# Three pairs of accumulator banks in turn, instead of two, in the feed-forwards of 512 tokens

## The chip, the cores and the metric

The kernel runs on one core of one Trainium2 chip. The metric is device microseconds of one execution of the whole program, taken as the median of several runs. Engines are named as in the profile: PE (TensorE matmuls), PEld (its weight loads), DVE (VectorE), ACT (ScalarE), POOL (GpSimd), SP (SyncE, which issues DMAs).

## The reference, cut to what matters

The reference is a four-layer network over 512 tokens of width 1024 in float32: a gated delta-rule layer, a dilated attention layer, and two layers of a second block that mixes neighbourhood attention, spatial gating and grouped attention, the first of them over 512 tokens and 256 context tokens. Every layer ends in a feed-forward with 2816 hidden columns. Cut down, the feed-forward is:

```
a, b = h @ w_in[:, :2816], h @ w_in[:, 2816:]     # "g" and "u" halves
x = x + (silu(a) * b) @ w_out                     # block 2 adds gains and norms
```

The second block also needs a modulation: for each of its two layers, `silu(c) @ w_mod[l] + b_mod[l]`, a vector times a 1024 x 6144 matrix, which depends on nothing but the inputs.

## The kernel before

Matrices are float32, and every operand is split into a high and a low part, so that a product is three matmuls (high by high, high by low, low by high). A matmul covers 128 rows, 128 contracted and up to 512 columns. Weights stream in slabs: SP loads one into `wraw`, ACT casts it to `whi`, POOL subtracts to make `wlo`. There are four `whi`/`wlo` pairs (names ending a and b), and a slab's pair is free for the next cast once PE has used it.

There are four feed-forwards, all in `ffn_core`. Three have 512 tokens (`nb` is 4): `ffn(0)`, `ffn(1)` and the one in `layer2(1)`. The one in `layer2(0)` has 768 tokens (`nb` is 6). In this text they are the first, second, fourth and third. The 22 hidden tiles of 128 columns are worked in three groups of 8, 8 and 6 (`FFN_GROUPS`). A group first computes its hidden tiles: a tile is 48 matmuls of 512 columns, 24 for `g` and 24 for `u`, into one pair of banks. Then `post` runs for the tile: ACT takes a tanh of `g` into `th`, DVE does a scalar_tensor_tensor and a tensor_tensor (both out `th`, in `th` and the banks) and so frees the pair, ACT casts to `hh` and POOL subtracts to `hl`. After the tiles comes the group's output: two halves of 512 columns, each with four accumulators (one for each block of 128 tokens), over n/2 weight slabs `c`. One slab for one block is six matmuls. An accumulator is added to `x` by `evac`, which is DVE work, and is free then. In the last group the second half goes through `tail`, block by block, with 18 matmuls each.

PSUM has eight banks: a ring of two for `psM`, two for `psS`, and two tiles of two banks for `psB`. In the feed-forwards of 512 tokens the hidden tiles take `psB` tiles in turn, each output half takes both `psB` tiles (`accs`: blocks 0 and 1 in one, 2 and 3 in the other), and the tail takes the two `psM` banks in turn. A `psB` tile comes free when all that was read from it has been read.

While the first two feed-forwards run, `modulation` computes the modulation on DVE, as a stream of lower priority: a 128 x 1024 piece of `w_mod` arrives in `mw` (a ring of three, issued from ACT's queue) and DVE multiplies and adds it into `macc`, 48 pieces in all, each for two vectors in the first feed-forward and for one or two in the second. After each eight pieces DVE transposes and reduces `macc` to `mpart`, PE does a small matmul of `mpart` into a `psS` bank, and DVE reads that into `modc`.

The order of the instructions on each engine is set when the program is built. `Weave` keeps an estimated clock for each engine, with costs of its own (`cost`), and steps a stream when the estimate says that its input is there; `Ring.get` advances the streams until a bank has been released in that order. A scheduler behind it places the instructions of each engine by a timeline of its own. Every engine then runs its queue in that order.

In the profile every instruction stands under line L138, the helper that records operations, so the rows are told apart by tile names: `b` is a `psB` tile, `m` a `psM` bank, `s` a `psS` bank.

Of the kernel before, what the change touches and what calls it, by code (L numbers as in the profile page):

```python
# [274 lines left out]
class Ring:  # L275
# [18 lines left out]
    def get(self):  # L294
        if self.held >= self.n:
            self.w.until(self.has)
            self.w.t["PE"] = max(self.w.t["PE"], self.time)
        return self._tile()
# [84 lines left out]
class Build:  # L383
# [108 lines left out]
            mm(ps, xh(k0 + k), lo[:, k], start=False, stop=last and k == nk - 1)  # L492
        self.w.tick()

    def gemm_b(self, arr, plan, keys, blocks, post, prio=0, base=0):

        P = PLANS[plan][0]
        n = P[keys[0]][4]
        held = [None] * len(keys)
        out = []  # L500
        for i, (b, rows, xh, xl, pre) in enumerate(blocks):
            if pre is not None:
                self.w.join(pre)
            ps = self.psM.get()[:rows, :n]
            for c, key in enumerate(keys):
                if held[c] is None:
                    held[c] = self.slabs.get(arr, key)
                self.mm_b(ps, xh, xl, held[c], P[key][1] - base, c == 0, c == len(keys) - 1)
                if i == len(blocks) - 1:
                    self.slabs.done(held[c])  # L510
            out.append(self.w.spawn(post(b, ps), prio))
        return out
# [591 lines left out]
    def accs(self, n, kinds="bbmm"):  # L1104
# [15 lines left out]
                out += [(t[:, :512], rel), (t[:, 512:], rel)]  # L1120
        return out

    def next_norm(self, side, row):

        es = ExitStack()
        self.n_act = getattr(self, "n_act", 0) + 1
        pool = self.open(es, f"act{self.n_act}", 1, side)
        xh = pool.tile([128, 8, 512], F32R, name="xh")
        xl = pool.tile([128, 8, 512], F32R, name="xl")
        gain = pool.tile([128, 1024], F32, name="row")  # L1130
        self.nc.sync.dma_start(gain, row.partition_broadcast(128))
        spare = FixedRing(self.w, [self.cx[:, 0], self.cx[:, 1]])
        return {"es": es, "xh": xh, "xl": xl, "st": [None] * 4, "gain": gain,
                "gen": lambda b: self.norm_rms(b, gain, xh, xl, self.nat, spare if b > 1 else None)}

    def tail(self, arr, plan, keys, blocks, evac, before, nxt, base=0):

        def post(b, ps):
            yield from evac(b, ps)
            if before:  # L1140
                yield before[b]
            nxt["st"][b] = self.w.spawn(nxt["gen"](b), 1)

        self.gemm_b(arr, plan, keys, blocks, post, 0, base)
        self.w.until(lambda: all(s is not None for s in nxt["st"]))


# [1 line left out]
    def ffn_core(self, wi, wo, segs, pre, setup, evac, nxt, grid=None):  # L1149

        nc, w, v = self.nc, self.w, self.nc.vector
        nb = sum(n for _, _, n in segs) // 128
        posts, mem = {}, {}

        def hidden(gi):
            if "one" not in mem:
                mem["one"] = setup()
                mem["th"] = Ring(w, mem["one"], "th", [128, nb * 128], 2)  # L1160
            if gi not in mem:
                mem[gi] = [(mem["one"].tile([128, 8, t], F32R, name=f"hh{i}", tag=f"hh{i}"),
                            mem["one"].tile([128, 8, t], F32R, name=f"hl{i}", tag=f"hl{i}"))
                           for i, (_, _, t) in enumerate(segs)]
            return mem[gi]

        def post(j, kk, pb, px, hs):
            rth = mem["th"]
            th = yield from rth.take()
            ps = [(pb[:, :512], pb[:, 512:], slice(0, 512))]  # L1170
            if px is not None:
                ps.append((px[:, :256], px[:, 256:], slice(512, 768)))
            for pg, _, t in ps:
                nc.scalar.activation(th[:, t], pg, AF.Tanh, scale=0.5)
            yield
            for pg, _, t in ps:
                v.scalar_tensor_tensor(th[:, t], th[:, t], 1.0, pg, ALU.add, ALU.mult)
            for _, pu, t in ps:
                v.tensor_mul(th[:, t], th[:, t], pu)
            self.psB.rel()  # L1180
            if px is not None:
                self.psM.rel()
            yield
            for (hh, hl), (_, _, t) in zip(hs, ps):
                oh, ol, s = hh[:, kk], hl[:, kk], th[:, t]
                if grid is not None:
                    g = "p (c s n) -> p n s c", "p (n s c) -> p n s c"
                    g = g if grid == "to" else g[::-1]
                    oh, ol = (x.rearrange(g[0], s=2, n=4) for x in (oh, ol))
                    s = s.rearrange(g[1], s=2, n=4)  # L1190
                nc.scalar.copy(oh, s)
                self.sub(ol, s, oh.bitcast(F32), "pool")
            rth.rel()

        def outs(half, pb, px, c0, c1):

            o = []
            if c0 < 512:
                xh, xl, _ = segs[0]
                c = slice(c0, min(c1, 512))  # L1200
                o.append((pb[:, 512 * half + c.start:512 * half + c.stop], lambda k: xh[:, k, c],
                          lambda k: xl[:, k, c]))
            if c1 > 512:
                yh, yl, n = segs[1]
                o.append((px[:, n * half:n * half + n], lambda k: yh[:, k], lambda k: yl[:, k]))
            return o

        def units(js, gi, k0, cuts):
            pbs = [(self.psB.get(), self.psM.get() if len(segs) > 1 else None) for _ in js]
            sl = {}  # L1210
            end = cuts[-1][1]
            for c0, c1, need in cuts:
                w.join(*need)
                for j, (pb, px) in zip(js, pbs):
                    for half, m in enumerate("gu"):
                        if (m, j) not in sl:
                            sl[m, j] = self.slabs.get(wi, (m, j))
                        self.mm_a(sl[m, j], outs(half, pb, px, c0, c1))
                        if c1 == end:
                            self.slabs.done(sl[m, j])  # L1220
                    if c1 == end:
                        posts[j] = w.spawn(post(j, j - k0, pb, px, hidden(gi)), 0)

        first = [(0, 256, pre[:2]), (256, 512, pre[2:4])]
        if nb > 4:
            first.insert(0, (512, 768, pre[4:]))
        for gi, (k0, n) in enumerate(FFN_GROUPS):
            js = list(range(k0, k0 + n))
            if not gi:
                units(js[:2], gi, k0, first)  # L1230
                js = js[2:]
            for j in js:
                units([j], gi, k0, [(0, 128 * nb, [])])

            def blk(b, hs=mem[gi]):
                (hh, hl), t = (hs[0], b * 128) if b < 4 else (hs[1], b * 128 - 512)
                return (lambda k: hh[:, k, t:t + 128]), (lambda k: hl[:, k, t:t + 128])

            ev = {}
            last = gi == len(FFN_GROUPS) - 1  # L1240
            for h in range(1 if last else 2):
                acc = self.accs(nb)
                order = list(range(nb))
                for c in range(n // 2):
                    w.join(*(posts.pop(j, None) for j in (k0 + 2 * c, k0 + 2 * c + 1)))
                    slab = self.slabs.get(wo, (gi, h, c))
                    for b in order:
                        self.mm_b(acc[b][0], *blk(b), slab, 2 * c, c == 0, c == n // 2 - 1)
                        if c == n // 2 - 1:
                            def ev0(gi=gi, b=b, h=h, acc=acc):  # L1250
                                yield from evac(gi, h, b, acc[b][0])
                                acc[b][1]()
                            ev[b] = w.spawn(ev0(), 0)
                    self.slabs.done(slab)
            if last:
                nxt = nxt()

                def ev1(b, ps):
                    yield from evac(gi, 1, b, ps)
                    self.psM.rel()  # L1260

                order = ([4, 5] if nb > 4 else []) + [0, 1, 2, 3]
                blocks = [(b, 128, *blk(b), None) for b in order]
                self.tail(wo, "ffn_out", [(gi, 1, c) for c in range(n // 2)], blocks, ev1, ev, nxt, k0)
        return nxt

    def ffn(self, i, after):
# [1308 lines left out]
```

## Time and profile before

| what | value |
|---|---|
| median of 3 runs | 3430.48 us (3426.53 to 3433.2) |
| profiled execution, its time | 3435.41 us |
| profiled execution, its span | 3433.6 us |
| PE busy | 3123.7 us, 91% of the span |
| DVE busy | 1735.3 us, 51% |
| ACT busy | 1257.0 us, 37% |
| POOL busy | 1440.1 us, 42% |
| mean granted TensorE clock | 0.947 of full speed |

The profiled execution's time is 4.93 us above the median and 1.81 us above its span. The first feed-forward runs from about 440 to 835 us of the span, the second from about 1205 to 1605 us, the third from about 2100 to 2630 us, the fourth from about 3050 to 3417 us.

### The profile page before, as it was taken

What the parts mean: (1) busy time and instruction counts of PE and PEld (TensorE: products, weight loads), DVE (VectorE), ACT (ScalarE), POOL (GpSimd) and SP (SyncE); (2) the same over time, 40 slices, a digit from 0 to 9 for tenths busy, and PEclk for the clock granted to TensorE, in tenths of its full rate; (3) what the DMA queues carried; (4) which work ended last, traced back from release to release, by engine and by line L of the source; (5) the groups of instructions that cost most, each with busy time, mean ns of one, the idle gap of its engine ahead of it and who ended that gap; (6) DMA issues with size and microseconds to landing.
All of it is one profiled execution on the core that took longest, in us unless ns stands there. A gap on an engine that the chain in (4) does not pass through costs nothing.

```text
span 3433.6 us, 44377 instructions
## 1 busy us (share of the span) xinstructions
PE 3123.7 (91%) x16596; PEld 2696.9 (79%) x16596; DVE 1735.3 (51%) x4221; ACT 1257.0 (37%) x2542; POOL 1440.1 (42%) x987
## 2 busy tenths in 40 slices
PE   7889888999999979999899897999998799869998
PEld 5678767777998767788788777888886789758886
DVE  6975598543464697213644755121015855751113
ACT  4443322222454422333455635212122555543322
POOL 2313344554323245555523325434445534355555
PEclk9989989999999989999999899999999899889999
DMA  3111255432222267323101212111111111242221
GB/s 106 63 33 62 87 178 172 158 122 95 68 63 68 74 210 244 124 94 118 51 24 44 74 41 80 62 65 65 62 67 53 52 39 54 66 122 94 98 98 68
DMA packets 99449, 301.82 MB, mean 88 GB/s; under 512 B 18673, under 2 KB 26017, under 8 KB 99233
## 3 DMA queue, kind: packets, MB, share of 16 engines
q1 hardware_dynamic: 74000, 236.36, 20.3%
q10 hardware_dynamic: 25232, 62.62, 5.7%
q8 instruction: 131, 2.15, 0.3%
q14 instruction: 86, 0.70, 0.1%
HBM read 290.98 MB, written 7.95 MB: 87 GB/s over the span
## 4 chain that ended last, share of the span: by engine, by line
PE 67%; DVE 23%; issue 4%; ACT 3%; DMA 2%; POOL 1%; ACTq 0%; SPq 0%; DVEq 0%; POOLq 0%
PE b L138 37%; PE m L138 24%; PE s L138 6%; DVE macc L138 5%; DVE rs_t L138 4%; DVE x L138 2%; DVE four L138 1%; ACT xn L138 1%; DMA mw<-w_mod 1%; DVE w2k L138 1%; DVE qrs L138 1%; DVE cx L138 1%; DVE tmp L138 1%; DVE T L138 1%; DVE th L138 1%
## 5 line engine op out<-in xcount | busy, mean ns | idle before, releaser
L138 POOL TENSOR_TENSOR wloa<-wrawa,whia 128x1024 fp32r<-128x1024 f32 (+2 forms) x164 | 391.9, 2391 | 617.8 <-ACT whia L138 375.3
L138 DVE SCALAR_TENSOR_TENSOR th<-th,b 128x512 f32<-128x512 f32 x88 | 60.3, 685 | 720.3 <-ACT th L138 720.3
L138 POOL TENSOR_TENSOR wlob<-wrawa,whib 128x1024 fp32r<-128x1024 f32 (+1 forms) x123 | 297.7, 2423 | 301.2 <-ACT whib L138 191.2
L138 ACT CAST whia<-wrawa 128x1024 fp32r<-128x1024 f32 (+2 forms) x164 | 168.3, 1027 | 401.8 <-PE b L138 162.0
L138 PE MATMUL b<-xh,whib 128*128 128x512 f32 (+1 forms) x768 | 288.6, 381 | 24.2 <-DVE th L138 16.8
L138 PE MATMUL b<-xh,whia 128*128 128x512 f32 (+1 forms) x768 | 286.7, 379 | 14.1 <-DVE th L138 12.1
L138 PE MATMUL b<-xl,whia 128*128 128x512 f32 (+1 forms) x768 | 285.2, 377 | 2.0 <-POOL xl L138 2.0
L138 PE MATMUL b<-xl,whib 128*128 128x512 f32 (+1 forms) x768 | 286.7, 379 | 0.0
L138 DVE SCALAR_TENSOR_TENSOR macc<-mw,cv,macc 128x1024 f32<-128x1024 f32 x140 | 247.9, 1812 | 16.1 <-DMA mw<-w_mod 15.6
L138 ACT CAST whib<-wrawa 128x1024 fp32r<-128x1024 f32 (+1 forms) x123 | 125.7, 1022 | 327.8 <-PE b L138 164.5
L138 POOL TENSOR_TENSOR wloa<-wrawb,whia 128x1024 fp32r<-128x1024 f32 (+2 forms) x61 | 141.6, 2321 | 189.5 <-ACT whia L138 120.2
L138 PE MATMUL m<-xh,whia 128*128 128x512 f32 (+2 forms) x520 | 188.3, 367 | 23.6 <-DVE T L138 10.1
L138 POOL TENSOR_TENSOR wlob<-wrawb,whib 128x1024 fp32r<-128x1024 f32 (+1 forms) x61 | 149.8, 2456 | 131.3 <-ACT whib L138 85.4
L138 POOL TENSOR_TENSOR hl<-th,hh 128x512 fp32r<-128x512 f32 (+1 forms) x110 | 151.8, 1389 | 101.4 <-ACT hh L138 97.0
L138 PE MATMUL b<-xh,wlob 128*128 128x512 f32 (+1 forms) x768 | 194.0, 373 | 0.0
L138 PE MATMUL b<-xh,wloa 128*128 128x512 f32 (+1 forms) x768 | 192.2, 372 | 0.0
L138 PE MATMUL m<-xl,whia 128*128 128x512 f32 (+2 forms) x520 | 184.9, 360 | 3.0 <-POOL xl L138 2.9
L138 PEld LDWEIGHTS b<-xh,whib 128*128 128x128 f32 x768 | 148.0, 193 | 47.3 <-issue 11.9
L138 PEld LDWEIGHTS b<-xh,whia 128*128 128x128 f32 x768 | 147.1, 191 | 36.4 <-issue 13.6
L138 PE MATMUL m<-whib,xh 128*128 128x512 f32 (+3 forms) x432 | 162.6, 379 | 13.8 <-ACT xh L138 12.8
L138 PE MATMUL m<-whia,xh 128*128 128x512 f32 (+3 forms) x440 | 170.8, 392 | 4.6 <-ACT xh L138 2.8
L138 PE MATMUL m<-whia,xl 128*128 128x512 f32 (+3 forms) x440 | 167.3, 383 | 0.4 <-DVE xl L138 0.3
(459 smaller groups left out, 8025.7 us busy)
## 6 DMA issues: line engine op xcount, KB each, us to landing
mw<-w_mod ACTq DMA_DIRECT2D x96, 512.0 KB, 4.3
wrawa<-ffn_w_in SPq DMA_DIRECT2D x60, 512.0 KB, 3.3
wrawa<-w_ffn_in SPq DMA_DIRECT2D x56, 512.0 KB, 3.3
wrawa<-gdn_w_in SPq DMA_DIRECT2D x32, 512.0 KB, 3.3
wrawb<-w_ffn_in SPq DMA_DIRECT2D x32, 512.0 KB, 3.3
wrawa<-w_ffn_out SPq DMA_DIRECT2D x32, 512.0 KB, 3.3
wrawb<-ffn_w_in SPq DMA_DIRECT2D x28, 512.0 KB, 3.3
wrawa<-ffn_w_out SPq DMA_DIRECT2D x28, 512.0 KB, 3.3
```

What stands on the lines that cost most here:

```text
L138: r = f(*a, **k)
```

## The change

Where `nb` is 4, the two `psM` banks become a third pair that takes turns with the two `psB` tiles. `pair()` hands out the pairs in a fixed rotation that runs on from one feed-forward to the next. Hidden tiles, both output halves and the tail all draw from it. A pair drawn for two accumulators is released when both have been added to `x`; in the tail, too, blocks 0 and 1 share a pair and so do blocks 2 and 3. The feed-forward of 768 tokens keeps its banks.

```diff
-    def gemm_b(self, arr, plan, keys, blocks, post, prio=0, base=0):
+    def gemm_b(self, arr, plan, keys, blocks, post, prio=0, base=0, get=None):
...
-            ps = self.psM.get()[:rows, :n]
+            ps = (get(b) if get else self.psM.get())[:rows, :n]
...
+    def pair(self):
+
+        i = self.turn = (getattr(self, "turn", -1) + 1) % 3
+        if i < 2:
+            t = self.psB.get()
+            return (t[:, :512], t[:, 512:]), self.psB.rel
+
+        def rel():
+            self.psM.rel()
+            self.psM.rel()
+
+        return (self.psM.get(), self.psM.get()), rel
+
+    def banks(self):
+
+        while True:
+            ps, rel = self.pair()
+            left = [2]
+
+            def half(left=left, rel=rel):
+                left[0] -= 1
+                if not left[0]:
+                    rel()
+
+            for p in ps:
+                yield p, half
...
-    def tail(self, arr, plan, keys, blocks, evac, before, nxt, base=0):
+    def tail(self, arr, plan, keys, blocks, evac, before, nxt, base=0, get=None):
...
-        self.gemm_b(arr, plan, keys, blocks, post, 0, base)
+        self.gemm_b(arr, plan, keys, blocks, post, 0, base, get)
...
-            ps = [(pb[:, :512], pb[:, 512:], slice(0, 512))]
+            (pg, pu), rel = pb
+            ps = [(pg, pu, slice(0, 512))]
...
-            self.psB.rel()
+            rel()
...
+        def wide():
+
+            if len(segs) == 1:
+                return self.pair(), None
+            t = self.psB.get()
+            return ((t[:, :512], t[:, 512:]), self.psB.rel), self.psM.get()
+
...
-                o.append((pb[:, 512 * half + c.start:512 * half + c.stop], lambda k: xh[:, k, c],
+                o.append((pb[0][half][:, c], lambda k: xh[:, k, c],
...
-            pbs = [(self.psB.get(), self.psM.get() if len(segs) > 1 else None) for _ in js]
+            pbs = [wide() for _ in js]
...
-                acc = self.accs(nb)
+                if nb > 4:
+                    acc = self.accs(nb)
+                else:
+                    bank = self.banks()
+                    acc = [next(bank) for _ in range(nb)]
...
+                bank, rels = self.banks(), {}
+
+                def get(b):
+                    if nb > 4:
+                        rels[b] = self.psM.rel
+                        return self.psM.get()
+                    ps, rels[b] = next(bank)
+                    return ps
+
                 def ev1(b, ps):
                     yield from evac(gi, 1, b, ps)
-                    self.psM.rel()
+                    rels[b]()
...
-                self.tail(wo, "ffn_out", [(gi, 1, c) for c in range(n // 2)], blocks, ev1, ev, nxt, k0)
+                self.tail(wo, "ffn_out", [(gi, 1, c) for c in range(n // 2)], blocks, ev1, ev, nxt, k0, get)
```

## Rows read from the trace of the kernel before

**Rows 1.** The page: busy time of each engine.

```profile
PE 3123.7 (91%) x16596; PEld 2696.9 (79%) x16596; DVE 1735.3 (51%) x4221; ACT 1257.0 (37%) x2542; POOL 1440.1 (42%) x987
```

**Rows 2.** Waits of PE, 430 to 860 us, then 1190 to 1640 us.

```profile
PE b L138 <- DVE th L138: 23.4, 8, 5.7
...
PE b L138 <- DVE x L138: 2.2, 2, 1.3
...
PE b L138 <- DVE th L138: 19.3, 4, 7.2
...
PE b L138 <- DVE x L138: 5.8, 1, 5.8
```

**Rows 3.** Windows: length, then PE, PEld, DVE, ACT, POOL busy, granted clock, DMA.

```profile
455.00:557.00 102.00, 84.67 (x391) 69.59 (x390) 100.59 (x69) 25.42 (x32) 52.23 (x23) 0.92 0.58 191
...
3064.00:3409.00 345.00, 345.00 (x1581) 288.43 (x1581) 60.15 (x88) 106.91 (x113) 200.85 (x97) 1.00 0.27 92
```

**Rows 4.** Timeline of PE, first feed-forward: start, us, instruction, idle before and releaser.

```profile
470.77 0.76 PE L138 MATMUL b<-xh,whib 128*128 128x512 f32 x1 [5.67 <-DVE th L138]
...
474.30 0.40 PE L138 MATMUL b<-xh,whib 128*128 128x512 f32 x1
...
509.90 0.76 PE L138 MATMUL b<-xh,whia 128*128 128x512 f32 x1 [3.71 <-DVE th L138]
...
553.38 0.77 PE L138 MATMUL b<-whib,hh 128*128 128x512 f32 x1 [4.88 <-DVE th L138]
...
578.61 0.47 PE L138 MATMUL b<-whib,hh 128*128 128x512 f32 x1 [1.27 <-DVE x L138]
...
626.00 0.47 PE L138 MATMUL b<-xh,whib 128*128 128x512 f32 x1 [3.22 <-DVE th L138]
...
637.62 0.47 PE L138 MATMUL b<-xh,whia 128*128 128x512 f32 x1 [0.46 <-DVE th L138]
...
703.90 0.50 PE L138 MATMUL b<-whib,hh 128*128 128x512 f32 x1 [2.40 <-DVE th L138]
...
720.25 0.31 PE L138 MATMUL s<-mpart,quart 128*32 128x16 f32 x8 [2.87 <-DVE mpart L138]
...
721.45 0.76 PE L138 MATMUL b<-whib,hh 128*128 128x512 f32 x1 [0.89 <-DVE x L138]
```

**Rows 5.** The chain that ended last: an undisturbed stretch of hidden tiles.

```profile
746.10 71.22 PE b L138 x314
```

**Rows 6.** Timeline of DVE, first feed-forward: posts of tiles 5, 6 and 7.

```profile
536.52 0.68 DVE L138 TENSOR_TENSOR th<-th,b 128x512 f32<-128x512 f32 x1
...
552.55 0.68 DVE L138 TENSOR_TENSOR th<-th,b 128x512 f32<-128x512 f32 x1
...
556.08 0.69 DVE L138 TENSOR_TENSOR th<-th,b 128x512 f32<-128x512 f32 x1
569.28 0.24 DVE L138 SCALAR_TENSOR_TENSOR modc<-s,bm 128x8 f32<-128x8 f32 x2 [12.51 <-PE s L138]
```

**Rows 7.** Timeline of PE, second feed-forward.

```profile
1249.27 0.77 PE L138 MATMUL b<-xh,whib 128*128 128x512 f32 x1 [7.25 <-DVE th L138]
...
1289.42 0.77 PE L138 MATMUL b<-xh,whia 128*128 128x512 f32 x1 [5.24 <-DVE th L138]
...
1338.34 0.80 PE L138 MATMUL b<-whib,hh 128*128 128x512 f32 x1 [6.59 <-DVE th L138]
...
1383.28 0.77 PE L138 MATMUL b<-xh,whib 128*128 128x512 f32 x1 [5.79 <-DVE x L138]
```

**Rows 8.** Timeline of DVE, second feed-forward: posts of tiles 6 and 7.

```profile
1323.23 0.68 DVE L138 TENSOR_TENSOR th<-th,b 128x512 f32<-128x512 f32 x1
...
1337.60 0.69 DVE L138 TENSOR_TENSOR th<-th,b 128x512 f32<-128x512 f32 x1
```

**Rows 9.** The costliest groups, then the timeline of ACT.

```profile
L138 DVE SCALAR_TENSOR_TENSOR macc<-mw,cv,macc 128x1024 f32<-128x1024 f32 x140 | 247.9, 1812 | 16.1 <-DMA mw<-w_mod 15.6
...
525.06 1.05 ACT L138 CAST whia<-wrawa 128x1024 fp32r<-128x1024 f32 x1 [4.47 <-DVE macc L138]
```

## The prediction, made before the change was built

> **What bounds the kernel now.** I read the page first. PE is busy for 91% of the span and no other engine for more than 51% [rows 1], so a gain has to come out of PE's idle time or its clock. Then I asked for PE's waits in the stretches of the feed-forwards, since the change touches nothing else. "PE b <- DVE th" is PE standing before a `psB` bank that a tile's post on DVE has not yet freed, and "PE b <- DVE x" is the same before an `evac`. In the first feed-forward they are 23.4 + 2.2 = 25.6 us, in the second 19.3 + 5.8 = 25.1 us [rows 2], 50.7 us in all. The fourth has none: PE is busy 345.00 of 345.00 us there [rows 3]. So only the first two can gain, and these are the two in which the modulation runs on DVE.
>
> The timeline of PE shows where the waits stand and that a long one costs more than itself. After 5.67 us of waiting at 470.77, eight matmuls take 474.30 - 470.77 = 3.53 us [rows 4], and in an undisturbed stretch eight take 8 x 71.22/314 = 1.81 us [rows 5]. So the clock is at its lower level for a moment and 1.7 us more is lost. The first matmul after a wait shows it by its own length: 0.76 to 0.80 us at the lower level, 0.47 to 0.50 otherwise [rows 4, 7]. Eight of these waits end in a matmul of the long kind [rows 4, 7], so the clock costs 8 x 1.7 = 13.6 us. The most that the change could give back is 50.7 + 13.6 = 64 us.
>
> Last I looked at what the late engine does meanwhile. From 455 to 557 us DVE is busy 100.59 of 102.00 us [rows 3]. The waits are thus not a hiccup that a deeper queue swallows: for these 100 us DVE, with the modulation in its queue, is the slower engine. One multiply-add into `macc` takes 1.81 us on average [rows 9], where the planner counts on 120 + 1.04 x 1024 = 1185 ns. The posts stand in DVE's queue behind them.
>
> **The change part by part.** It adds no arithmetic, no copy and no DMA. A third pair lets PE begin a tile when the post three tiles back is done instead of two, so it may lead DVE by one tile more. An undisturbed tile is 48 x 71.22/314 = 10.9 us [rows 5]. I assume that DVE keeps its order and, where it is full, its times.
>
> *First feed-forward, first group.* The rotation gives the group's eight tiles pairs 0,1,2,0,1,2,0,1, its first half pairs 2 and 0, its second half 1 and 2. PE is through tiles 0 and 1 at 470.77 - 5.67 = 465.1 [rows 4]. Tiles 2 to 5 then need 4 x 10.9 us, to 508.7. Tile 6 needs post 3, which released tile 5 at 509.9 [rows 4], 1 us later, and with tile 7 and 0.5 us for modulation matmuls the tiles end near 532. Blocks 0 and 1 of the first half wait for post 5 instead of 6: 537.2 instead of 553.23 [rows 6]. Blocks 2 and 3 wait for post 6 instead of 7: 553.23 instead of 556.77. So the waits saved inside the tiles come back in front of blocks 2 and 3, because DVE gets to post 6 no earlier. What remains is the work left at 553.3. Before, the half ended at 578.61 - 1.27 = 577.3 [rows 4]. After, if PE's order goes slab by slab, 12 of 96 matmuls are done and 84 follow at 0.227 us, plus 1.7 us for the clock: 553.3 + 19.1 + 1.7 = 574.1, a gain of 3.2. If blocks 0 and 1 run ahead by some 30 matmuls, as they do now, 66 remain: 553.3 + 15.0 + 1.7 = 570.0, a gain of 7.3. I take 5.
>
> *Its second half and second group.* The second half draws tile 7's pair, free since post 7, so the 1.27 us before it go. Tiles 10 and 11 waited 3.22 and 0.46 us for posts 8 and 9 [rows 4]. They now need posts 7 and 8 or an accumulator pair long empty, so these go as well: 5 + 1.27 + 3.22 + 0.46 = 10. DVE drains in between, so nothing returns here. In the group's output the 2.40 us at 703.90 go, but a modulation matmul behind them waits for `mpart` until 720.25 [rows 4], and that hangs on DVE work begun by PE itself; its 2.87 us grow by 2.40. The 0.89 us behind it go. Sum: 11 us. The bounds are 9 (3.2 in the first step, the rest as it is) and 20 (7.3, and the `mpart` matmul placed so late that its 2.4 + 2.9 + 1.7 us vanish).
>
> *Second feed-forward.* Tiles 0 and 1 end at 1249.27 - 7.25 = 1242.0 [rows 7]; four tiles more, to 1285.6. Tile 6 needs post 3, which released tile 5 at 1289.4 [rows 7]: a wait of 3.8 and 1.7 for the clock. The tiles end at 1289.4 + 21.8 + 1.7 = 1312.9. Blocks 2 and 3 need post 6, at 1323.9, instead of post 7, at 1338.29 [rows 8]. But the half's last slab multiplies tile 7 itself, and that cannot be had before post 7 and its cast, near 1340. Its 24 matmuls take 5.4 us and perhaps 1.7 for the clock, so the half ends at 1346 to 1347.5. Before, the second half ran right up to the wait at 1383.28 - 5.79 = 1377.5 [rows 7], and 96 x 0.227 us before that, the first half ended near 1355.5. The gain is about 8. Then the 5.79 us before tile 8 and its slow matmuls go, because tile 8 draws a pair emptied a half earlier: 7.5. Sum: 15.5 us, bounded below by 8 (only one of the two) and above by all of 19.3 + 5.8 + 4 x 1.7 = 32.
>
> *Tail and the other feed-forwards.* The tail gives each pair back when two blocks are through instead of one. A block of the tail is 18 matmuls, 4.1 us, and four blocks now have four banks without reuse, so nothing waits for that. The waits of 430 to 860 us name no wait before an `m` bank, so I take nothing. `psM` now carries hidden tiles, and the next layer's projections draw from it; at the end of the first two feed-forwards the last draws are pairs 2 and 0, and 0 and 1, emptied at the same `evac` as before. I take nothing here.
>
> *Weights.* If PE leads by more, it needs its slabs earlier. ACT casts them in order behind its `mw` issues, which wait for DVE: the cast at 525.06 had waited 4.47 us for `macc` [rows 9]. It is the `u` slab of tile 7, which in the schedule above starts at 526. So it is just in time and costs nothing, but the slabs would hold PE soon if the banks did not.
>
> Sum: 11 + 15.5 = 26.5 us, from 3435.41 to 3408.9 us. The median of the runs is 4.93 us below the profiled execution, so 3404.0 us.
>
> **A rule against it.** The trace says that PE waits 50.7 us for banks [rows 2] while DVE has 1.4 us free in 102 [rows 3]. The Trainium skill, "TensorE: Matmul & The Clock Gate", section "HAM oscillation — how this bites in real kernels", reports of a kernel already arranged to keep PE busy that double-buffering PSUM gave no further gain (126.6 against 125.5 us). By that the sum would be 0 and the time 3430 us. Against it stands that DVE does run empty later, 12.51 us at 569.28 waiting for PE [rows 6]: each engine waits for the other in turn, which more banks can loosen. It is the second rival.
>
> **The rivals.**
>
> 1. *Nearly all waits go.* If the scheduler, seeing free banks, places posts ahead of `macc` work, then DVE is late with the modulation only, which nothing needs until the last group. The gain is 40 to 64 us: 3366 to 3390. For it speaks that all of DVE's 100.59 us in the first group is queue order, not need. Against it speaks that the same scheduler puts `macc` work between a tile's two DVE instructions now.
> 2. *The wait only moves.* DVE is the slower engine, and what is saved in front of tiles is paid in front of blocks 2 and 3 and the `mpart` matmuls, in both feed-forwards. For it speaks the first step above, where 3 to 7 us of 13 survive. The gain is under 7 us: 3424 to 3437.
> 3. *Slower.* Today both `psB` tiles are asked for before a half's first matmul, which puts tile 7's post in the queue at that point. Afterwards the half asks for pairs long free, and post 7 is forced only by the last slab. If the planner lays more `macc` work before it in the three halves that overlap the modulation (two groups of the first, one of the second), each multiply-add costs 1.81 us of wait before the last slab. At 5 of them in each half, 3 x 5 x 1.81 = 27 us, the gain is gone; at 8 it is 43 us and the time 3430.5 - 26.5 + 43 = 3447 us.
> 4. That the rotation does nothing is excluded: the banks asked for differ from the third tile on.
>
> **How the numbers follow.** The bounds of the two sums give a gain of 17 (9 + 8) to 52 us (20 + 32); the forecast takes 7 to 40 of it, 3390 to 3424, so that it meets the rivals on both sides, with a chance of 0.58. Rival 1 has 0.17, rival 2 0.15, rival 3 0.10. About 0.2%, 6.9 us, is what a measurement of this kernel can tell. The forecast and rival 1 are faster: 0.75. Rival 2 is the same: 0.15. Rival 3 is slower: 0.10. The range leaves out rival 3 (0.10), the far end of rival 1 (some 0.05) and the slow edge of rival 2 (some 0.03): 3374 to 3433.
>
> **What would show it.** In the changed trace the waits of PE for `th` at tiles 2 to 5 of both feed-forwards should be gone, at 470.77, 1249.27 and their like. One wait of 5 us or more should stand in the first output half of each, ended by post 6 or, in the second, by the cast of tile 7. The waits before tile 8 of the second and before tile 10 of the first should be gone. DVE should still be full to about 557. The fourth feed-forward should take as long as now. I am wrong if DVE's posts come at other times than now, earlier (rival 1) or later (rival 3), since all terms hang on their times; or if PE waits for `wloa`, `whia` and their kin instead.

## The result and the profile after

The changed kernel takes 3386.35 us (3383.95 to 3393.49, 4 runs) against 3431.41 us: a ratio of 0.9874, 95% interval 0.9855 to 0.9893, or 45 us. In a later session, beside the first experiments, the same kernel took 3395.78 us against 3429.31 us: 0.9906 (0.9892 to 0.9921), or 33.5 us. The forecast was 3404, with a range of 3374 to 3433.

The profiled execution has a span of 3382.1 us. The page, answering to [rows 1]:

```profile
PE 3106.0 (92%) x16596; PEld 2687.0 (79%) x16596; DVE 1729.1 (51%) x4221; ACT 1255.2 (37%) x2542; POOL 1437.9 (43%) x987
```

The waits of PE around the first feed-forward, 430 to 800 us, answering to [rows 2] (total, times, longest):

```profile
PE b L138 <- DVE th L138: 12.6, 2, 12.2
PE m L138 <- DVE x L138: 5.1, 1, 5.1
PE m L138 <- ACT whib L138: 2.3, 1, 2.3
PE m L138 <- POOL wlob L138: 1.7, 1, 1.7
```

And around the second, 1150 to 1600 us:

```profile
PE b L138 <- POOL wlob L138: 5.1, 1, 5.1
PE b L138 <- DVE th L138: 3.0, 2, 2.3
...
PE b L138 <- ACT whib L138: 2.6, 1, 2.6
```

The 50.7 us of waits for DVE are 20.7 now: 12.6 + 5.1 and 3.0. A new kind stands beside them, 11.7 us for weight slabs. The timeline of PE shows where they are, answering to [rows 4, 7]:

```profile
521.89 0.50 PE L138 MATMUL m<-whib,hh 128*128 128x512 f32 x1 [2.33 <-ACT whib L138]
...
524.80 1.22 PE L138 MATMUL m<-wlob,hh 128*128 128x512 f32 x2 [1.72 <-POOL wlob L138]
...
540.81 0.79 PE L138 MATMUL b<-whib,hh 128*128 128x512 f32 x1 [12.23 <-DVE th L138]
...
701.39 0.80 PE L138 MATMUL m<-whib,hh 128*128 128x512 f32 x1 [5.09 <-DVE x L138]
...
1246.93 0.64 PE L138 MATMUL b<-xh,whib 128*128 128x512 f32 x1 [2.30 <-DVE th L138]
...
1273.18 0.50 PE L138 MATMUL b<-whib,hh 128*128 128x512 f32 x1 [2.61 <-ACT whib L138]
...
1279.45 1.22 PE L138 MATMUL b<-wlob,hh 128*128 128x512 f32 x2 [5.05 <-POOL wlob L138]
```

One long wait is left in the first output half. It stands before the `b` bank of blocks 2 and 3, after the 12 matmuls of blocks 0 and 1 on the two `m` banks. The timeline of DVE, answering to [rows 6, 8], has what ends it: the second instruction of post 6, which stands behind two multiply-adds as before.

```profile
535.60 4.55 DVE L138 SCALAR_TENSOR_TENSOR macc<-mw,cv,macc 128x1024 f32<-128x1024 f32 x2
540.08 0.68 DVE L138 TENSOR_TENSOR th<-th,b 128x512 f32<-128x512 f32 x1
...
543.60 0.69 DVE L138 TENSOR_TENSOR th<-th,b 128x512 f32<-128x512 f32 x1
557.32 0.24 DVE L138 SCALAR_TENSOR_TENSOR modc<-s,bm 128x8 f32<-128x8 f32 x2 [13.04 <-PE s L138]
...
1283.19 0.67 DVE L138 TENSOR_TENSOR th<-th,b 128x512 f32<-128x512 f32 x1
...
1296.15 0.67 DVE L138 TENSOR_TENSOR th<-th,m 128x512 f32<-128x512 f32 x1
```

The windows, answering to [rows 3]: DVE is as full in the first group as before, and the fourth feed-forward has nothing to gain or lose.

```profile
455.00:545.00 90.00, 73.40 (x313) 58.74 (x312) 88.14 (x63) 22.04 (x29) 46.16 (x21) 0.89 0.59 189
...
3020.00:3365.00 345.00, 345.00 (x1553) 286.80 (x1551) 64.83 (x96) 105.47 (x107) 201.59 (x98) 1.00 0.29 91
```

To compare stretches I measure between starts of the tanh of hidden tiles on ACT, which every trace shows once for each hidden tile of the feed-forwards of 512 tokens (and twice in the third, where a tile has two parts). The table is worked out from those rows, in us. A is the first feed-forward from tile 0 to tile 16. B runs from there over its last group, its tail and the dilated layer to tile 0 of the second. C is the second feed-forward, tile 0 to 16. D is the rest, to the last tile of the fourth. The first column is the start of the first tile's tanh. Each row is one execution, and not always a typical one: that of the tiles-only kernel was 14 us faster than the median of its runs (3396.77 against 3410.81), that of the order alone 8 us (3343.34 against 3351.48).

```
                          start      A       B       C        D
before                    459.4   297.6   479.3   293.7   1854.4
before, again             455.2   294.5   475.6   295.2   1856.0
after                     447.5   285.9   461.5   276.5   1860.9
after, again              456.9   285.9   461.5   276.7   1864.2
tiles only                451.6   287.9   475.1   281.7   1849.6
halves only               459.1   292.6   475.6   277.2   1856.9
after, old tail           455.4   285.8   477.3   274.9   1864.9
tail only                 455.4   295.6   465.9   299.5   1855.2
before, light DVE         459.4   257.0   474.6   270.7   1855.6
after, light DVE          450.6   256.2   462.6   257.5   1860.0
after, order              447.9   258.5   462.2   262.5   1860.7
after, order and cost     459.1   258.8   479.1   259.6   1867.7
after, order and spacing  457.0   267.8   463.6   263.5   1861.9
before, order and spacing 457.0   275.7   474.9   261.7   1859.0
```

From the means of the first two rows to those of the next two, A falls by 10.2, B by 15.9 and C by 17.9, together 44.0, and D rises by 7.4. The prediction took B as nothing. It took D as nothing too, and D lies the other way.

### The profile page after: what moved, and what is told of

It is laid out like the page before. It is cut to its first block, busy times and chain, and to the rows that moved or that the text cites. A ratio compares the mean times of both kernels' runs of the same rounds, so it can differ in the third digit from the quotient of the medians.

```text
span 3382.1 us, 44404 instructions
## 1 busy us (share of the span) xinstructions
PE 3106.0 (92%) x16596; PEld 2687.0 (79%) x16596; DVE 1729.1 (51%) x4221; ACT 1255.2 (37%) x2542; POOL 1437.9 (43%) x987
## 4 chain that ended last, share of the span: by engine, by line
PE 54%; DVE 11%; ACT 3%; issue 2%; POOL 1%; DMA 1%; ACTq 0%; SPq 0%; DVEq 0%; POOLq 0%
PE b L138 26%; PE m L138 23%; PE s L138 4%; DVE rs_t L138 3%; ACT xn L138 1%; DVE x L138 1%; DVE w2k L138 1%; DVE four L138 1%; DVE qrs L138 1%; DVE macc L138 1%; DMA mw<-w_mod 0%; POOL wloa L138 0%; ACT w2k L138 0%; DVE bst L138 0%; DVE xn L138 0%
## 5 line engine op out<-in xcount | busy, mean ns | idle before, releaser
L138 PE MATMUL m<-xh,whia 128*128 128x512 f32 (+1 forms) x760 | 272.3, 365 | 18.1 <-DVE tmp L138 4.5
L138 PE MATMUL m<-xl,whia 128*128 128x512 f32 (+1 forms) x760 | 268.4, 359 | 3.0 <-POOL xl L138 2.9
L138 PE MATMUL b<-xh,whib 128*128 128x512 f32 (+1 forms) x624 | 230.9, 376 | 4.3 <-DVE th L138 2.6
L138 PE MATMUL b<-xl,whib 128*128 128x512 f32 (+1 forms) x624 | 229.9, 375 | 0.0
L138 PE MATMUL b<-xh,whia 128*128 128x512 f32 (+1 forms) x528 | 198.6, 380 | 2.1 <-ACT xh L138 2.1
L138 PE MATMUL b<-xl,whia 128*128 128x512 f32 (+1 forms) x528 | 198.1, 380 | 2.0 <-POOL xl L138 2.0
L138 PE MATMUL m<-xh,wloa 128*128 128x512 f32 (+1 forms) x760 | 186.2, 354 | 0.0
L138 PEld LDWEIGHTS m<-xh,whia 128*128 128x128 f32 x760 | 146.7, 194 | 48.5 <-issue 14.4
L138 PEld LDWEIGHTS m<-xl,whia 128*128 128x128 f32 x760 | 146.3, 193 | 29.9 <-POOL xl L138 3.2
L138 PE MATMUL m<-whib,xl 128*128 128x512 f32 (+3 forms) x432 | 161.9, 377 | 1.6 <-POOL xl L138 1.6
```

Source lines behind the costliest of these rows:

```text
L138: r = f(*a, **k)
```

## The experiments

**The two kernels again.** No edit. The two traces differ by 12 us before the first instruction that the change touches, and the order of the instructions up to there is the same.

> The kernel before, profiled a second time. The changed program reached the end of its first two hidden tiles at 453 us of its span, the one before at 465 us, with the same order of instructions up to there. Theory A (chance between executions): the second profile of the kernel before ends them anywhere from 453 to 465 us, and 12 us of the difference of the two profiles is none of the change's. Theory B (the changed program runs its first layer faster): 465 us again, within 2 us. Time 3426 to 3434 us either way.

> The changed kernel, profiled a second time, as the partner for the runs beside it. Theory A: its first tiles end anywhere from 453 to 465 us and its time is 3384 to 3393 us. Theory B: 453 us again, within 2 us.

Measured: 3431.62 us for the kernel before (ratio to its other runs 1.0005, 0.9987 to 1.0023), 3395.78 us for the changed one. The first tile starts at 455.2 and 456.9 us. With 459.4 and 447.5 of the first traces, the four lie anyhow: theory A. Those 12 us are chance, and the first pair of traces shows too much by that. A, B and C agree within 3.7 us between the two traces of the kernel before and within 0.2 us between those of the changed one.

**Hidden tiles alone on three pairs.** The halves ask for both `psB` tiles again, the tail for `psM`.

```diff
-                if nb > 4:
-                    acc = self.accs(nb)
-                else:
-                    bank = self.banks()
-                    acc = [next(bank) for _ in range(nb)]
+                acc = self.accs(nb)
+                if nb == 4:
+                    self.turn = (self.turn + 2) % 3
...
-                    ps, rels[b] = next(bank)
-                    return ps
+                    rels[b] = self.psM.rel
+                    return self.psM.get()
```

> Hidden tiles draw from three pairs; output halves take both psB tiles and the tail the two psM banks, as before the change. Theory of the prediction (DVE reaches each post no earlier, so the waits before the tiles come back before the half): blocks 0 and 1 of a half wait for post 6 again, and only the waits at tiles 10 and 11 of the first feed-forward go. The gain is 0 to 8 us: 3421 to 3431 us, and waits of 10 us or more stand in front of the first halves. Rival (the waits before tiles are a loss of their own; they are 28.6 of the 50.7 us): a gain of 20 to 30 us, 3400 to 3411 us.

Measured: 0.9956 (0.9940 to 0.9973), 3410.81 us: a gain of 18.5 us. That is above the 8 I allowed and just short of the rival's 20, and the time itself lies at the edge of the rival's range, so the time does not decide between the two. The profile does for the first group. The timeline of PE has what the theory says of the first group: no wait at its tiles, and all of it again before the half.

```profile
543.91 0.77 PE L138 MATMUL b<-whib,hh 128*128 128x512 f32 x1 [20.94 <-DVE th L138]
```

The half began at 553.38 before; 451.6 - 459.4 = -7.8 us of shift would put that at 545.6, so the tiles' lead bought 1.7 us there. A falls by 8 nevertheless, most of it in the second group, where DVE drains. C falls by 13, which I had not expected. There the rotation of this run starts one pair later (its 34 draws leave 34 mod 3 = 1), so tiles 5 and 6 hold the two `psB` tiles and tile 7 the `psM` pair. The half then needs posts 5 and 6 even when it asks for both `psB` tiles. My expectation missed where the rotation stands at this point.

**Output halves alone.** Tiles and tail as before. A half of the first two groups takes the `psM` pair and one `psB` tile.

```diff
-            if len(segs) == 1:
-                return self.pair(), None
...
-                if nb > 4:
+                if nb > 4 or last:
                     acc = self.accs(nb)
                 else:
+                    self.turn = 1 - h
                     bank = self.banks()
```

> Hidden tiles take the two psB tiles in turn, as before the change, and the tail its psM banks; the output halves of the first two groups take the psM pair and one psB tile, so that they never need the last tile's pair. Theory of the prediction: the half is where the lead is worth something, so this alone gives most of it. First feed-forward: 5 us at the first half, 1.3 before the second, 1 to 3 in the second group; second feed-forward: 8 us at the half, 7.5 at tile 8. The gain is 18 to 25 us: 3406 to 3413 us. The waits before tiles 2 to 5 stand as before. Rival (waits before tiles count for themselves): 10 us at most, 3421 us or more.

Measured: 0.9956 (0.9941 to 0.9971), 3411.88 us: a gain of 17.4 us, just under the 18 I expected and far above the rival's 10. C falls by 17.2, all that the whole change gives there, with the waits of 5.2 and 7.2 us before the second feed-forward's tiles in place. In A the wait before the half is short now, and blocks 2 and 3 have it:

```profile
553.02 0.50 PE L138 MATMUL b<-whib,hh 128*128 128x512 f32 x1 [2.11 <-DVE th L138]
```

In C, then, a wait before a tile is no loss by itself, because the next half has to wait for the same engine anyway. A falls by only 3.4 here.

**The tail, taken out and alone.** First the changed kernel with single `psM` banks in its tail, the phase kept; then the kernel before with blocks 2 and 3 of the tail on a `psB` tile.

```diff
-                    ps, rels[b] = next(bank)
-                    return ps
+                    rels[b] = self.psM.rel
+                    return self.psM.get()
```

```diff
+                def get(b):
+                    if nb > 4 or b < 2:
+                        rels[b] = self.psM.rel
+                        return self.psM.get()
+                    if not own:
+                        own.extend(self.accs(2))
+                    ps, rels[b] = own[b - 2]
+                    return ps
```

> The changed kernel with the tail back on single psM banks in turn; tiles and halves keep the three pairs and their rotation. Theory A (the tail's banks are worth something that the prediction took as nothing: with blocks 2 and 3 on a psB tile, psM is free for the next layer's projections while the tail still runs): the wait of 5.1 us for xl after the first tail is back, PE is busy some 77 of 85 us around it instead of 84, and the time is 8 to 12 us above the changed kernel's 3386 to 3396: 3396 to 3407 us. Theory B (the stretch after the first feed-forward differs by chance): as the changed kernel, 3384 to 3396 us.

> The kernel before with one part of the change: in the tail blocks 0 and 1 take the two psM banks and blocks 2 and 3 one psB tile. Tiles and halves as before. Theory A: the wait of 5.1 us for xl after the first tail goes, with 3 us for qn and the clock; 3430 - 10 = 3420 us, within 4. All waits of the feed-forwards stay. Theory B: 3430 us, within 4.

Measured: 3410.35 us (0.9949, 0.9931 to 0.9967) with the old tail, some 15 to 24 us above the changed kernel; 3418.87 us (0.9965, 0.9949 to 0.9981) with the tail alone, 12 us under the kernel before. Both are theory A, the first 3 us above its range. B is 477.3 with the old tail and 465.9 with the tail alone. The windows of 85 us around the first tail show the same two values of PE busy twice (length, PE, PEld, DVE, ACT, POOL, clock, DMA). Before, after, after with the old tail, and the tail alone:

```profile
805.00:890.00 85.00, 76.82 (x358) 66.95 (x357) 44.28 (x107) 27.22 (x52) 27.50 (x13) 0.94 0.26 84
```

```profile
776.00:861.00 85.00, 84.21 (x407) 74.78 (x406) 42.94 (x109) 30.62 (x57) 31.55 (x15) 1.00 0.29 92
```

```profile
789.00:874.00 85.00, 76.82 (x354) 66.83 (x353) 44.29 (x107) 26.74 (x49) 27.87 (x14) 0.92 0.27 87
```

```profile
799.00:884.00 85.00, 84.22 (x407) 75.80 (x406) 41.59 (x107) 31.59 (x59) 30.62 (x15) 1.00 0.26 83
```

With blocks 2 and 3 on a `psB` tile PE gets 50 matmuls more through in the same 85 us, and at the full clock. The wait of 5.1 us for `xl`, PE's transposes of the next norm standing behind one another, is gone from the trace; `m` matmuls of the dilated layer run between these transposes, on the `psM` banks that blocks 2 and 3 no longer hold. The waits of PE in the last two of these windows, with the old tail and then with the tail alone:

```profile
PE s L138 <- DVE xl L138: 5.1, 1, 5.1
PE s L138 <- DVE qn L138: 3.1, 1, 3.1
```

```profile
PE s L138 <- DVE qn L138: 0.8, 1, 0.8
```

The tail of the second feed-forward gives nothing of that kind. The profile of the tail alone has 5 us more in C than the kernel before, which stays open.

**Without DVE's load.** Both kernels with the multiply-adds cut to 64 columns (the other 960 are left out of the modulation). On the page this takes DVE's busy time from 1735.3 [rows 1] to 1553.8 us in the kernel before.

```diff
-                        v.scalar_tensor_tensor(acc[:, s], wt, cs, acc[:, s], ALU.mult, ALU.add)
+                        v.scalar_tensor_tensor(acc[:, s, :64], wt[:, :64], cs, acc[:, s, :64],
+                                               ALU.mult, ALU.add)
```

> The kernel before, with the multiply-adds of the modulation done on 64 of 1024 columns (its values are left out of the computation otherwise), so that DVE is no longer full. Theory of the prediction (the waits for banks exist only because DVE is late): no wait for th of over 1 us is left in the two feed-forwards, and with 50.7 us of waits and 13.6 us of clock gone the time is 3355 to 3380 us. Rival (two pairs are too few by themselves): waits for th of 2 us and more stand in the second group of the first feed-forward and elsewhere, 3400 us or more.

> The changed kernel with the same light modulation. Theory of the prediction, with the tail as theory A has it: only the tail's part is left of the change, 8 to 12 us less than the light kernel before, 3345 to 3370 us. Rival (a third pair is worth its tile of lead whatever DVE does): 25 us or more less than the light kernel before.

Measured: 3368.99 us with two pairs, 3345.70 us with three. A is 257.0 and 256.2: in the first feed-forward, where DVE is not late now, two pairs do as well as three, and 39 us of the 296 were its lateness. The difference of 23 us is more than the 12 I allowed and near the 25 of the rival. B has 12 of it, the tail. C has 13, and most of that is one wait of the light kernel before, where I had expected none of over 1 us. The timeline of PE, then of DVE:

```profile
1277.10 0.80 PE L138 MATMUL b<-whib,hh 128*128 128x512 f32 x1 [8.55 <-DVE th L138]
```

```profile
1269.85 1.88 DVE L138 SCALAR_TENSOR_TENSOR macc<-mw,cv,macc 128x64 f32<-128x64 f32 x1 [2.32 <-DMA mw<-w_mod]
1275.45 0.28 DVE L138 SCALAR_TENSOR_TENSOR macc<-mw,cv,macc 128x64 f32<-128x64 f32 x1 [3.72 <-DMA mw<-w_mod]
1275.65 0.68 DVE L138 SCALAR_TENSOR_TENSOR th<-th,b 128x512 f32<-128x512 f32 x1
1276.36 0.69 DVE L138 TENSOR_TENSOR th<-th,b 128x512 f32<-128x512 f32 x1
```

The last tile's post stands in DVE's queue behind multiply-adds that wait for their `mw` piece. DVE is idle and the post is late all the same. So here it is the order of the queue that makes PE wait, and not DVE's work.

**The order itself.** Whether this holds under the full load too was open, so the last runs change DVE's order and leave its work whole. Every multiply-add is placed behind the latest post that the planner has emitted.

```diff
-                v.tensor_mul(th[:, t], th[:, t], pu)
+                self.posted = v.tensor_mul(th[:, t], th[:, t], pu)
...
-                    if k == 0:
-                        with self.tc.issue_after(normed.ins):
+                    with self.tc.issue_after(self.posted.ins):
+                        if k == 0:
                             v.tensor_scalar(acc[:, s], wt, cs, None, ALU.mult)
-                    else:
-                        v.scalar_tensor_tensor(acc[:, s], wt, cs, acc[:, s], ALU.mult, ALU.add)
+                        else:
+                            v.scalar_tensor_tensor(acc[:, s], wt, cs, acc[:, s], ALU.mult, ALU.add)
```

> The changed kernel with one thing more: every multiply-add of the modulation is placed on DVE behind the latest post that the planner has emitted, so that it can no longer slip in between a tile's two post instructions or ahead of a post. Theory of the prediction (what is left of the waits is DVE's queue order, not DVE's work): the wait of 12 us before blocks 2 and 3 of the first half shrinks below 5 us, the 5 us for an evac at 701 us and the waits for weights in the second feed-forward shrink too; 15 to 30 us less than the changed kernel: 3356 to 3381 us. Rival (DVE's work in the first group is too much in any order): within 7 us of the changed kernel, 3380 to 3400 us.

Measured: 3351.48 us (0.9773, 0.9746 to 0.9799), 35 to 44 us under the changed kernel, more than the 15 to 30 that I expected, and the fastest of the kernels that do all the work. Its window of the first group:

```profile
455.00:557.00 102.00, 102.00 (x464) 83.75 (x463) 96.96 (x71) 27.10 (x32) 62.27 (x26) 1.00 0.63 197
```

DVE does 96.96 us of work there, nearly as much as before [rows 3], and PE never waits: 102.00 of 102.00 at the full clock, where it was 84.67. A and C are within 2.3 and 5 us of those of the changed kernel without DVE's load.

Two runs more spread the modulation further, by the planner's cost for a multiply-add or by spacing its steps:

```diff
-            return e, (75 if n < 64 else 120) + 1.04 * n
+            return e, 1812 if op == "scalar_tensor_tensor" and n == 1024 else (75 if n < 64 else 120) + 1.04 * n
```

```diff
-                    w.cur.ready += 1800
+                    w.cur.eng = None
+                    w.cur.ready += 1000
```

> As the run before it, and the planner counts 1812 ns, the trace's mean, for a multiply-add of 1024 columns instead of 1185, so that it lays three of them between two posts instead of four. Theory: no wait for th over 2 us is left in either feed-forward; 25 to 35 us less than the changed kernel, 3351 to 3371 us, unless the modulation is now late for the last group. Rival: as with the order alone, or slower.

> As the order alone, and the modulation's steps are spaced 1000 ns apart in the planner in place of the 1800 ns that DVE's own clock overrode. Theory: as with the cost corrected, 3351 to 3371 us.

Measured: 3375.54 us (0.9837, 0.9816 to 0.9858) with the cost, 3360.26 us (0.9795, 0.9771 to 0.9818) with the spacing: under the changed kernel, and worse than the order alone, as the rival had it; the time with the cost lies above its range too. With the cost A and C are as good, but B is back at 479.1. The last multiply-add of the first modulation now ends at 795 us instead of 729, where the tail's norms want DVE. The waits of PE from 765 to 1160 us:

```profile
PE s L138 <- DVE xn L138: 3.4, 1, 3.4
PE b L138 <- DVE x L138: 3.4, 2, 2.9
...
PE s L138 <- DVE mpart L138: 2.5, 1, 2.5
```

None of the three stands there with the order alone. That the late end of the modulation is what makes them was not tested by itself. With the spacing it ends at 781 us, the three are not there either, and B is 463.6.

**Two pairs with the order mended.** The kernel before with the order and the spacing.

> The kernel before, with two pairs, and the same order and spacing of the modulation as the run before it. Theory (the waits for banks came from DVE's order, and the tail's banks are a separate gain of some 11 us): nearly all of the 50.7 us of waits and their clock are gone without a third pair, 3430 - 55 = 3375 us, within 8, and the run with three pairs is 8 to 15 us below it. Rival (the third pair is needed for its lead): 3400 us or more.

Measured: 3379.70 us (0.9852, 0.9831 to 0.9874), 52 us under the kernel before and below the changed kernel, with two pairs. Three pairs with the same order and spacing take 3360.26, 19 us less, where I expected 8 to 15. The two profiles, 14 us apart, have 11 us more for two pairs in B, the tail, and 8 in A, where two pairs leave a half waiting for the other half's `evac`:

```profile
697.98 0.76 PE L138 MATMUL b<-whib,hh 128*128 128x512 f32 x1 [8.13 <-DVE x L138]
```

That `evac` stands on DVE behind four multiply-adds (689.69 to 696.64 us), since the edit puts multiply-adds behind posts only. Whether two pairs would still lose the 8 us with the `evac` ahead of them was not run, nor two pairs with the order and without the spacing.

## Why the prediction was right, and where it was off

**Which feed-forwards gain.** Right for the feed-forwards: the fourth is full before and after, and the first two gain, in A and C. About a third of the gain, in B, comes with the first one's tail and the layer behind it (below).

**DVE reaches each post no earlier.** Right for the posts that end the waits, and all else hung on them. From tile 0's tanh to the end of post 6 the first feed-forward takes 553.2 - 459.4 = 93.8 us before and 540.8 - 447.5 = 93.3 after. In the second, post 7 comes 101.9 us after tile 0 before and 1296.8 - 1195.0 = 101.8 after. Not every post kept its time: counted from tile 0, posts 2 and 5 of the first feed-forward come 7.5 and 6.2 us earlier, and post 5 of the second 3.4 us later. No long wait hung on these.

**"DVE is the slower engine" for these 100 us.** Wrong as a reason. With the order changed, DVE has 96.96 us of work in a window of 102 us and PE never waits. What made the posts late was their place in its queue. The modulation only ends later: its last reduction ends 287 us after tile 0's tanh instead of 261.

**First feed-forward, 11 us.** Right: 10.2, in part by luck. Less the 11.9 us by which this trace is early, the first half ends where the slab-by-slab sum put it: 561.9 + 11.9 = 573.8 against 574.1. The `mpart` matmul, whose wait I let grow to 5.3 us, is no longer the one that waits. PE stands 5.09 us for an `evac` at 701.39 instead. That costs the same, but the sum did not have this wait.

**Second feed-forward, 15.5 us.** Right: 17.9. The half ends where the sum put it: at 1306.2 us, which is 1347.6 on the clock of the trace before (its tile 0 comes 41.4 us later), against 1346 to 1347.5. The wait of 5 us or more that I expected before the last tile's matmuls is not there. A wait of 5.05 us for a weight slab stands earlier in the half instead, and PE then stands only 0.45 us for tile 7's `hl`, at 1300.87.

**Weights just in time, at no cost.** Wrong as a forecast of what PE waits for, and one of the signs of being wrong that the prediction named; harmless for the sum as far as the traces show. PE waits 4.05 and 7.66 us for slabs in the two first halves. The 4.05 us lie ahead of the wait for post 6, the 7.66 us ahead of 0.69 us for post 6 and the 0.45 us for tile 7, and those would have ended no earlier, so the slabs change the kind of the wait more than the time. How much they cost by themselves was not measured.

**"Nothing waits for that" in the tail: the step that failed.** I looked for waits before the tail's own banks and found none. What mattered was who wants the banks afterwards. I took nothing where the term is 12 to 16 us: B falls by 15.9, and with and without the new tail it differs by 11.6 (tail alone against the mean of the two traces before) and 15.8 (old tail against the changed kernel). With 12 to 16 us for it, less the 7 us that D gives back for reasons I could not find, the sum is 31 to 35 us instead of 26.5, against 33.5 and 45 measured. So the forecast came as near as it did also because two terms were missing that point opposite ways.

**The rivals.** Rival 1, that nearly all waits go because posts move ahead of `macc` work, did not happen by the change: the posts that end the waits kept their times. It happened when the order was changed by hand, and it was worth 35 to 44 us more, as the rival's argument said ("queue order, not need"). Rival 2 is the right account of the first group, where 20.94 us come back before the half if the tiles alone are freed, but not of the sum. Rival 3 did not occur.

The Trainium skill, "TensorE: Matmul & The Clock Gate", section "HAM oscillation — how this bites in real kernels", on PSUM double-buffering without gain: the runs disagree for the whole change, at 0.9874, and agree with it in A once DVE's load is taken away, 257.0 against 256.2 us.

## What to carry to other kernels

When an engine waits for a bank, look at what stands ahead of the releasing instruction in the late engine's queue. In the first group here a further pair hid one tile of lateness, and the next point that needed the late result collected it again. Moving the background work behind the release gave as much as the banks and more. When banks change hands, ask who draws from the ring next: a third of this gain came from the following layer's projections, which found `psM` free. Background work that is spread too thinly can run into the next stage: with the planner's corrected cost the kernel lost 24 of the 35 to 44 us that the order had given, most of it there.

## What the runs showed that was not expected

Two executions of one program differ in stretches that have the same instruction order: the first layer ended up to 12 us apart in four profiles, and ten runs of the kernel before in one session reached from 3416.51 to 3441.86 us. A difference of 10 us between two traces must be found again in a second pair before it is explained. The stretch from the second feed-forward's last group on, D, is some 7 us longer with the change in both its profiles (1860.9 and 1864.2 against 1854.4 and 1856.0). The table speaks against chance: D is 1860.0 to 1867.7 in all seven rows in which both the tiles and the output halves draw from three pairs, and 1854.4 to 1859.0 in the five rows in which both keep two. With only one of them on three pairs it is 1849.6 and 1856.9. What in the change costs these 7 us was not found.
